# A LoRA router on one core: eight rows per load instead of four in the middle of the input stream

## The chip, the core and the metric

The kernel runs on one core of one Trainium2 chip. The metric is the device time of one execution in microseconds (us); the kernel before takes 88.85 us, the median of three runs (88.81 to 88.88). The profiled execution took 88.78 us, and its profile covers a span of 87.0 us from the first to the last instruction. All times inside the kernel below are counted from the start of that span.

## The reference

```python
def reference(x, router_weights):           # x: 16 x 512 x 1024, float32; weights: 1024 x 8
    logits = np.matmul(x, router_weights)
    exp_logits = np.exp(logits - np.max(logits, axis=-1, keepdims=True))
    return (exp_logits / np.sum(exp_logits, axis=-1, keepdims=True)).astype(np.float32)
```

There are 8192 rows of 1024 numbers. Each row is multiplied with a thin matrix of eight columns, and a softmax over the eight results is written out. The input is 33.6 MB and the output 0.26 MB.

## The kernel before

**Layout.** The 8192 rows are spread over 128 partitions, 64 consecutive rows to each (`J = 64`). "Row j" below means the 128 rows that stand at place j of their partitions, a tile of 128 x 1024. Since the 64 rows of a partition lie one after the other in memory, several rows of one partition are one contiguous piece.

**Loading.** `LOADS` (L38) says how many rows each load brings. Load 0 (rows 0 to 3) comes as float32 from the SyncE queue in two transfers of two rows (L65), and ScalarE casts it to bfloat16 row by row (L74). All other loads are issued by GpSimd (L76), and the transfer itself casts to bfloat16 on the way. Each load has a tile of its own, `x_1`, `x_2` and so on, so no load ever waits for a buffer. Row 63 comes last in two pieces, `xe_0` of six and `xe_1` of two column blocks (L86). The compiler's framework gives the GpSimd transfers eight semaphores in turn, so GpSimd's ninth transfer waits until the first has landed, the tenth for the second, and so on: eight transfers are in flight at most.

**Working on a row.** TensorE contracts over partitions, so each row tile must first be turned. `turn` (L162) transposes the eight 128x128 blocks of a row into PSUM by matmuls with the identity. `evict` (L173) copies the result back to SBUF as `xT`: on VectorE alone for rows below `NEAR` = 54, and from there on five blocks on VectorE and three on ScalarE. `project` (L114) then makes eight small matmuls with `xT` as the stationary side, which give the eight logits of each row. It runs two rows behind the transposes (one row from row 54 on).

**Order.** The loop over j is written out under a manual schedule, so each engine runs its instructions in exactly the order of the program: transposes of row j, projection of row j-2, then filler. For rows 24 to 59 `fill` (L104) adds matmuls of 128x512 on a constant tile whose result nobody reads: two per row for rows 24 to 47, one per row for rows 48 to 59. There is no filler after row 59. The softmax of a group of eight rows is cut in five steps, and one step is done after each row's eviction (L134 to L149).

**End.** After the loop come row 62, which comes in a load of its own, and row 63 from the two `xe` pieces. A transfer named `mark` waits for `xe_0`, then the first 54 rows of output are stored (L195); the last ten rows follow after the last softmax (L224).

Of the kernel before, what the change touches and what calls it, by code (L numbers as in the profile page):

```python
# [10 lines left out]
def kernel(  # L11
# [23 lines left out]
    ALU = mybir.AluOpType  # L35


    LOADS = [4] * 13 + [2, 2, 2] + [1] * 5  # L38
    LAST_LOADS = [6, 2]
    GROUPS = [8] * 6 + [6, 8, 1, 1]  # L40
    assert sum(LOADS) == J - 1 and sum(LAST_LOADS) == KO and sum(GROUPS) == J
    DONE = sum(GROUPS[:7])
# [11 lines left out]
    with tc.manual_schedule():  # L54
# [7 lines left out]

        x_f32 = const.tile([P, LOADS[0], D], fp32)
        for k in range(0, LOADS[0], 2):
            nc.sync.dma_start(out=x_f32[:, k:k + 2, :], in_=x_rows[:, k:k + 2, :])  # L65
# [3 lines left out]
        j0 = 0  # L69
        for i, r in enumerate(LOADS):  # L70
            xb = xpool.tile([P, r, D], bf16, name=f"x_{i}", tag=f"x_{i}")
# [183 lines left out]
```

## Time and profile before

| what | before |
|---|---|
| device time | 88.85 us |
| span of the profile | 87.0 us |
| TensorE matmul busy | 63.8 us (73% of the span) |
| VectorE busy | 48.1 us (55%) |
| ScalarE busy | 12.4 us (14%) |
| GpSimd busy | 12.9 us (15%) |
| queue of the GpSimd transfers | 3168 packets, 15.73 MB written, 88.3% of the 16 DMA engines' span |
| HBM read | 33.59 MB |

The megabytes of the queue are counted on the side that writes, in bfloat16; the reading side is twice as large. Busy shares are averages over the whole span. The first 40 us, in which TensorE waits for most loads, and the last 30 us, in which it has filler to do, are different stages. The granted clock of TensorE is 0.934 of full speed on average, which is also a mixture of stretches at full and at half clock.

### The profile page before, as it was taken

The page shows a single profiled execution, that of the slowest core. Times are in us where ns is not written, and L with a number is a line of the kernel's source. Part 1 is how long each engine was busy: PE and PEld are TensorE (multiplying, and loading weights), DVE is VectorE, ACT ScalarE, POOL GpSimd, SP SyncE. Part 2 cuts the span into 40 slices and gives each one's busy share as a digit, 9 for nine tenths or more (in the row PEclk, how much of TensorE's full clock was granted, in tenths as well). Part 3 has the DMA queues.
Part 4 walks back from the last instruction along what each step waited for, and adds up shares of the span by engine and source line. Part 5 has one row for each costly group of instructions (what it writes and reads, how often), then busy time and mean ns, then how long its engine had stood idle before and what let it go on. Part 6 is the DMA issues. An engine that isn't in the chain of part 4 may idle for free.

```text
span 87.0 us, 2427 instructions
## 1 busy us (share of the span) xinstructions
PE 63.8 (73%) x1092; PEld 53.6 (62%) x1092; DVE 48.1 (55%) x112; ACT 12.4 (14%) x25; POOL 12.9 (15%) x29
## 2 busy tenths in 40 slices
PE   0408004999396926949999998989898999997730
PEld 0407004999296926947777775757575888795620
DVE  0303300699576663723677677746676589563760
ACT  3235009000100010000010001000100003454540
POOL 5990002020010202020010202020010222000000
PEclk9999999999956999555999999999999999999997
DMA  3899999999999999999999999999999999999520
GB/s 60 328 358 286 260 249 222 222 211 230 196 222 211 222 215 211 226 207 215 218 215 226 200 226 215 207 226 207 226 207 198 220 213 210 202 210 211 88 102 19
DMA packets 3773, 18.26 MB, mean 210 GB/s; under 512 B 556, under 2 KB 940, under 8 KB 1972
## 3 DMA queue, kind: packets, MB, share of 16 engines
q0 software_dynamic: 3168, 15.73, 88.3%
q1 hardware_dynamic: 580, 2.36, 7.3%
q8 instruction: 8, 0.13, 0.5%
q10 hardware_dynamic: 16, 0.03, 0.2%
q14 instruction: 1, 0.01, 0.0%
HBM read 33.59 MB, written 0.26 MB: 389 GB/s over the span
## 4 chain that ended last, share of the span: by engine, by line
DMA 89%; POOL 3%; issue 2%; DVE 1%; PE 1%; ACT 0%; POOLq 0%
DMA x<-in_x_dram 75%; DMA xe<-in_x_dram 14%; POOL x L76 2%; POOL filler L81 1%; DVE xT L173 0%; PE lg L114 0%; PE pt L162 0%; POOL ident masks.py:199 0%; ACT ev_last L215 0%; POOL ident masks.py:197 0%; DVE ssum_last L219 0%; DVE low L214 0%; DVE ssum_last L220 0%; DVE outv L221 0%; POOLq L239 0%
## 5 line engine op out<-in xcount | busy, mean ns | idle before, releaser
L173 DVE COPY xT<-pt 128x1024 bf16<-128x1024 bf16 (+2 forms) x65 | 42.0, 652 | 31.8 <-PE pt L162 31.6
L162 PE MATMUL pt<-identity,x 128*128 128x128 bf16 x504 | 43.4, 236 | 16.0 <-ACT x L74 8.1
L162 PEld LDWEIGHTS <-x 128*128 128x128 bf16 x504 | 34.6, 105 | 25.8 <-DMA x<-in_x_dram 10.9
L114 PE MATMUL lg<-w_bf,xT 128*128 128x8 bf16 x512 | 22.7, 168 | 0.3 <-DVE xT L173 0.2
L114 PEld LDWEIGHTS <-xT 128*128 128x128 bf16 x512 | 20.7, 99 | 0.5 <-DVE xT L173 0.5
L104 PE MATMUL spare<-filler 128*128 128x512 bf16 x60 | 19.2, 384 | 0.0
L76 POOL DMA_DIRECT2D x<-in_x_dram x20 | 10.7, 543 | 56.2 <-DMA x<-in_x_dram 55.4
L140 ACT ACTIVATE ev<-ex 128x64 f32<-128x64 f32 (+1 forms) x8 | 2.0, 255 | 56.2 <-DVE ex L137 56.2
L173 ACT COPY xT<-pt 128x384 bf16<-128x384 bf16 (+1 forms) x10 | 4.7, 467 | 5.1 <-PE pt L162 4.9
L74 ACT CAST x<-x_f 128x1024 bf16<-128x1024 f32 x4 | 4.0, 1042 | 8.5 <-DMA x_f<-in_x_dram 8.5
L104 PEld LDWEIGHTS <-filler 128*128 128x128 bf16 x60 | 4.1, 96 | 0.0
L92 PE MATMUL lg<-ident,w 8*128 8x8 f32 x8 | 1.0, 254 | 3.1 <-POOL ident masks.py:199 3.1
L92 PEld LDWEIGHTS lg<-ident,w 8*128 8x128 f32 x8 | 1.0, 198 | 3.1 <-POOL ident masks.py:199 3.1
L89 DVE CAST identity<-ident 128x128 bf16<-128x128 f32 x1 | 0.5, 512 | 3.0 <-POOL ident masks.py:199 3.0
L134 DVE TENSOR_REDUCE mx<-lg 128x8 f32<-128x64 f32 (+1 forms) x8 | 1.7, 213 | 0.5 <-PE lg L114 0.5
L137 DVE TENSOR_TENSOR ex<-lg,mx 128x64 f32<-128x64 f32 (+1 forms) x8 | 1.7, 213 | 0.0
L149 DVE TENSOR_TENSOR outv<-ev,inv 128x64 f32<-128x64 f32 (+1 forms) x8 | 1.7, 212 | 0.0
L143 DVE TENSOR_REDUCE ssum<-ev 128x8 f32<-128x64 f32 (+1 forms) x8 | 1.7, 208 | 0.0
L86 POOL DMA_DIRECT2D xe<-in_x_dram x2 | 1.1, 527 | 3.9 <-DMA x<-in_x_dram 3.9
L146 DVE RECIPROCAL inv<-ssum 128x8 f32<-128x8 f32 (+1 forms) x8 | 1.5, 191 | 0.0
L74 ACT ACT_TABLE_LOAD x1 | 1.3, 1283 | 1.3 <-PEq L239 1.3
L162 PE MATMUL pt<-identity,xe 128*128 128x128 bf16 x8 | 0.6, 222 | 0.2 <-DMA xe<-in_x_dram 0.2
(14 smaller groups left out, 3.4 us busy)
## 6 DMA issues: line engine op xcount, KB each, us to landing
x<-in_x_dram POOLq DMA_DIRECT2D x12, 1024.0 KB, 35.4
x_f<-in_x_dram SPq DMA_DIRECT2D x2, 1024.0 KB, 8.4
x<-in_x_dram POOLq DMA_DIRECT2D x3, 512.0 KB, 33.9
x<-in_x_dram POOLq DMA_DIRECT2D x5, 256.0 KB, 20.6
out_dram<-outv SPq DMA_DIRECT2D x1, 216.0 KB, 1.9
xe<-in_x_dram POOLq DMA_DIRECT2D x1, 192.0 KB, 11.8
xe<-in_x_dram POOLq DMA_DIRECT2D x1, 64.0 KB, 9.7
out_dram<-outv SPq DMA_DIRECT2D x1, 40.0 KB, 1.5
```

Source lines behind the costliest of these rows:

```text
L74: nc.scalar.copy(xb[:, k, :], x_f32[:, k, :])
L76: nc.gpsimd.dma_start(out=xb[:], in_=x_rows[:, j0:j0 + r, :])
L92: nc.tensor.transpose(w_ps[:, n, :], w8[:, :, n], ident[0:KO, 0:KO])
L104: nc.tensor.matmul(spare[:], lhsT=filler[:, 0:P], rhs=filler[:], start=True, stop=True)
L114: nc.tensor.matmul(logits[g][:, k, :], lhsT=xT[:, i, :], rhs=w_bf[:, k0 + i, :], start=(k0 + i == 0), stop=(k0 + i == KO - 1),)
L134: nc.vector.reduce_max(mx[:, :, 0], lg, axis=X)
L137: nc.vector.tensor_tensor(out=ex[:], in0=lg, in1=mx[:].broadcast_to([P, n, N]), op=ALU.subtract)
L140: nc.scalar.activation(ev[:], ex[:], func=Exp)
L143: nc.vector.reduce_sum(ssum[:, :, 0], ev[:], axis=X)
L149: nc.vector.tensor_tensor(out=outv[:, a:a + n, :], in0=ev[:], in1=inv[:].broadcast_to([P, n, N]), op=ALU.mult)
L162: nc.tensor.transpose(pt[:, c, :], xb[:, (i + c) * P:(i + c + 1) * P], identity[:])
L173: copy(out=xT[:], in_=pt[:, 0:n, :])
```

## The change

One line is changed.

```diff
-    LOADS = [4] * 13 + [2, 2, 2] + [1] * 5
+    LOADS = [4] + [8] * 5 + [4] * 2 + [2, 2, 2] + [1] * 5
```

Rows 4 to 43 came in ten loads of four rows (16 KB contiguous per partition in memory, 8 KB after the cast). They now come in five loads of eight rows (32 KB contiguous, 16 KB after the cast). The aim is fewer and longer pieces for the DMA engines. Rows 0 to 3 and everything from row 44 on are loaded in the same pieces as before. GpSimd issues 17 transfers instead of 22; with eight in flight at most, rows 4 to 53 are now in flight at the start, where it was rows 4 to 35. The order of the instructions on TensorE, VectorE and ScalarE is the same as before; only the load that a row waits for is another one.

## The prediction

> **What bounds the kernel now.** I read the chain that ended last first. It is nearly all transfers:
>
> ```profile
> DMA 89%; POOL 3%; issue 2%; DVE 1%; PE 1%; ACT 0%; POOLq 0%
> DMA x<-in_x_dram 75%; DMA xe<-in_x_dram 14%; POOL x L76 2%; POOL filler L81 1%; DVE xT L173 0%; PE lg L114 0%; PE pt L162 0%; POOL ident masks.py:199 0%; ACT ev_last L215 0%; POOL ident masks.py:197 0%; DVE ssum_last L219 0%; DVE low L214 0%; DVE ssum_last L220 0%; DVE outv L221 0%; POOLq L239 0%
> ```
>
> So the kernel ends when the last input lands, plus a short tail. How close is TensorE behind? GpSimd's timeline is a clock of the landings: each issue after the eighth waits for a load and starts 0.28 us after it (columns: start, duration, engine, line, operation, count, idle before).
>
> ```profile
> 48.23 0.53 POOL L76 DMA_DIRECT2D x<-in_x_dram  x1 [4.34 <-DMA x<-in_x_dram]
> 53.16 0.53 POOL L76 DMA_DIRECT2D x<-in_x_dram  x1 [4.40 <-DMA x<-in_x_dram]
> 58.01 0.53 POOL L76 DMA_DIRECT2D x<-in_x_dram  x1 [4.32 <-DMA x<-in_x_dram]
> 62.90 0.53 POOL L76 DMA_DIRECT2D x<-in_x_dram  x1 [4.37 <-DMA x<-in_x_dram]
> ```
>
> Rows 32-35 have landed at 47.95, rows 40-43 at 57.73, rows 44-47 at 62.62: four rows per 4.87. TensorE's timeline over the same stretch, rows 40, 41 and 44:
>
> ```profile
> 57.77 0.62 PE L162 MATMUL pt<-identity,x 128*128 128x128 bf16 x8 [0.36 <-DMA x<-in_x_dram]
> 58.23 0.34 PE L114 MATMUL lg<-w_bf,xT 128*128 128x8 bf16 x8
> 58.43 0.59 PE L104 MATMUL spare<-filler 128*128 128x512 bf16 x2
> 58.86 0.61 PE L162 MATMUL pt<-identity,x 128*128 128x128 bf16 x8
> ...
> 62.66 0.51 PE L162 MATMUL pt<-identity,x 128*128 128x128 bf16 x6 [0.40 <-DMA x<-in_x_dram]
> ```
>
> This carries the prediction. A row costs TensorE 58.86 - 57.77 = 1.08 us, filler included; four cost 4.33 of the 4.87 us in which they arrive. It waits only 0.4 us per load, so in this stage it can make up 0.54 us per load and no more. The last stage, same view, rows 48, 61, 62 and 63:
>
> ```profile
> 67.57 0.62 PE L162 MATMUL pt<-identity,x 128*128 128x128 bf16 x8 [0.41 <-DMA x<-in_x_dram]
> ...
> 79.97 0.62 PE L162 MATMUL pt<-identity,x 128*128 128x128 bf16 x8 [0.47 <-DMA x<-in_x_dram]
> ...
> 81.31 0.61 PE L162 MATMUL pt<-identity,x 128*128 128x128 bf16 x8
> 82.16 0.64 PE L162 MATMUL pt<-identity,xe 128*128 128x128 bf16 x8 [0.24 <-DMA xe<-in_x_dram]
> ```
>
> TensorE still waits for loads at rows 61 and 63: it is caught up. Last, the clock, by stretches (length, busy time of each engine, then PEclk):
>
> ```profile
> 17.46:24.29 6.83, 5.34 (x134) 5.25 (x131) 5.44 (x11) 0.26 (x1) 0.99 (x2) 1.00 1.01 212
> 24.29:27.70 3.41, 3.30 (x53) 3.21 (x49) 2.67 (x7) 0.00 (x0) 0.07 (x1) 0.50 1.04 216
> 27.70:31.11 3.41, 2.74 (x64) 2.65 (x64) 2.55 (x6) 0.00 (x0) 0.53 (x1) 1.00 1.02 214
> 41.35:82.10 40.75, 38.26 (x662) 29.66 (x659) 27.45 (x65) 5.20 (x14) 4.22 (x8) 1.00 1.04 209
> ```
>
> **What the Trainium skill says.** "DMA: Bandwidth & Descriptors", section Anatomy of one DMA: a GpSimd transfer has about 2 us of fixed cost, mostly the receipt of its last write. Here that is hidden, as later loads stand queued behind: in the trace's packet records an undisturbed DMA engine finishes its four-row loads every 4.867 us, two-row loads every 2.457, one-row loads every 1.252. The differences, 2.410 and 1.205, are exactly proportional to rows, which leaves 0.047 us fixed per load. Same page, section Why small descriptors are slow: an overhead of some three cycles per packet. The trace agrees that it is small: the 0.047 covers eight packets and a completion. Same page, section Queues, rings and completion order: an engine alternates between queues packet by packet. The trace agrees: from 5.2 to 12 us packets of the second float32 transfer and of `x_1` alternate, one pair per 0.925 us. "TensorE: Matmul & The Clock Gate", Part 1: the clock is set by how busy TensorE was in a free-running window of about 3.4 us, else it is halved. The 3.41 us steps above agree. The window 27.70 to 31.11 with 2.74 us busy kept the clock; the one ending at 24.29, with an idle gap of 1.49, lost it.
>
> **The change, part by part.**
>
> *Removed: five loads.* 5 x 0.047 = 0.24 us off the stream, all of it gone by the time row 43 lands; later loads keep their spacing. The lower bound is 0, if the hardware cuts 32 KB pieces in two. The upper bound comes from packet durations: an 8 KB packet takes 625 ns and a 4 KB one 324, so some 23 ns are not proportional; 40 packets fewer per engine x 23 ns + 5 completions x 22 ns = 1.0 us. I take 0.24, since intervals count the overlap of packets and durations do not. GpSimd's 5 x 0.53 us of issuing saved cost nothing before: it waited 55.4 us at L76.
>
> *Start.* Packets of `x_1` become twice as long (about 1.2 us), so each pair takes about 1.5 and the second float32 transfer lands near 17.3 instead of 13.09. ScalarE's casts (1.04 each) and TensorE's rows 2 and 3 move behind it; rows 4-11 follow at about 20.7 and, at 0.65 to 1.07 each, end by 26 to 29. Rows 12-19 come at 28.2, so this is hidden.
>
> *Moved: the first row of each pair of loads waits for the second four.* Rows 4, 12, 20, 28 and 36 become available about 4.9 us later than before. For the first four blocks the slack swallows it: eight rows arrive per 9.69 us. Rows 20-27 may run partly at half clock, as rows 20-26 do now. For rows 28-35 the work is 8 x 1.08 = 8.65, so they begin at 47.95 - 0.2 and end by 56.4, before the next block.
>
> *The last block is not swallowed.* Rows 36-43 are free at 57.73 - 0.24 + 0.04 = 57.53; row 36 began at 52.92 before. From there TensorE has, by the spacing of its own rows where they did not wait:
> - rows 36-47: 12 x 1.08 = 12.97 (rows 44-47 have landed at 62.4, before their turn at 66.2)
> - rows 48-53: six in 67.57 to 72.78 = 5.21 (one filler each, 0.87 per row)
> - row 54, where one extra projection is flushed: 1.07
> - rows 55-59: five at 0.87 = 4.34
> - row 60, without filler: 0.68, from 0.45 transposes and 0.2 projection
> - row 61, whose projection waits for its own eviction: 1.34 (79.97 to 81.31)
>
> The sum is 25.61, so row 62 begins at 57.53 + 25.61 = 83.14 instead of 81.31: 1.83 later. All loads have landed by then (row 62 before 81.2, `xe` before 82.5), so TensorE never waits again after 57.5. The wait for data at the end is replaced by a queue of work: behind row 36 all later rows queue on TensorE, and VectorE, ScalarE and the last store wait for them. VectorE does not bind in the block (0.69 copy + about 0.13 softmax per row against 1.08 or 0.87). The tail after row 62 is the same chain, paced by ScalarE's copies from 82.17 on. 88.85 + 1.83 = 90.7.
>
> **Rivals.** *Half clock in the backlog, slower still.* Before row 36 TensorE idles about 0.9 us, leaving 2.5 busy in a window, between the 2.74 that kept the clock and the 1.92 (3.41 - 1.49) that lost it. If it is lost, one window of 3.41 us runs rows at 1.90 (rows 24 to 25 now) instead of 1.08: 3.41 x (1 - 1.08/1.90) = 1.5 us more, 92.2. Against it: a gap split by a window's edge counts less, and continuous work follows.
>
> *The stream alone sets the end: faster.* If TensorE caught up, only the shorter stream would show: 88.85 - 0.24 = 88.6, or 87.9 at the upper bound. For it speaks the chain, 89% transfers. Against it: this needs 1.8 us of slack after row 36, and 25.6 us of fixed work up to row 62 against the 23.4 us from row 43's landing to row 62's (57.73 to 81.17) show none; nothing in the change shortens filler.
>
> *A wash.* The saving is 1.0 us and TensorE recovers another 0.8: 88.9. The bound alone gives 57.73 - 1.0 and thus 89.9.
>
> **How the numbers follow.** Late TensorE at full clock, 90.7: 0.70. Half clock, 92.2: 0.20. Stream alone, 88.6: 0.08. Wash: 0.02. The range runs from the first case with the upper saving (89.9, less 0.2 for the landing of row 43, which hangs on the slowest DMA engine, 1.4 us behind the first) to the half-clock case with no saving at all (92.4): 89.7 to 92.4. It leaves out the last two cases.
>
> **What would show it.** Right: landings of rows 43 and 47 some 0.24 us earlier; row 36 at about 57.5; no wait of TensorE for loads after that; row 62 near 83.1; transfers no longer dominating the end of the chain. Wrong: gaps for loads at rows 56 to 63 (the stream still bounds); eight-row landings not 9.69 us apart (the saving is mis-sized); half clock after 57 us (the second case).

## The result and the profile after

The changed kernel takes 90.38 us (median of five runs, 90.14 to 90.44) against 88.84 us before (five runs, 88.81 to 88.88). The ratio is 1.0166, with a 95% interval of 1.0153 to 1.0180: 1.54 us slower, where 1.83 was forecast. The profiled execution has a span of 88.5 us. In the experiments below, two executions (91.77 us with four long loads, 93.73 us with one long load alone) fell in a slower state; the ratios leave them out.

The chain that ended last, by engine and by line:

```profile
DMA 49%; PE 39%; POOL 3%; DVE 2%; issue 2%; another core or an unknown queue 1%; ACT 0%; POOLq 0%
DMA x<-in_x_dram 49%; PE pt L162 18%; PE spare L104 12%; PE lg L114 8%; POOL x L76 2%; DVE xT L173 1%; POOL filler L81 1%; POOL ident masks.py:199 0%; ACT ev_last L215 0%; DVE mx L134 0%; DVE ex L137 0%; POOL ident masks.py:197 0%; DVE ssum_last L219 0%; DVE ssum_last L220 0%
```

Transfers had 89% of it; now they have 49%, and TensorE has 39%: transposes, filler and projections. `xe` is gone from the chain. The pieces of the chain in order of time change from the input to TensorE at 47.66 us, which is row 28. But the view does not name what ended the wait before row 36:

```profile
56.48 0.94 another core or an unknown queue
57.47 0.62 PE pt L162 x8
```

The load of rows 36 to 43 landed at 57.42 (below), so the wait was for this load, and TensorE's own work leads to the end from row 36 on. The 39% are too high by rows 28 to 35.

GpSimd's timeline again tells the landings (each issue follows one by 0.28 us; the lines tell of rows 28-35, 36-43 and 44-47):

```profile
47.90 0.53 POOL L76 DMA_DIRECT2D x<-in_x_dram  x1 [9.19 <-DMA x<-in_x_dram]
57.70 0.53 POOL L76 DMA_DIRECT2D x<-in_x_dram  x1 [9.27 <-DMA x<-in_x_dram]
63.41 0.53 POOL L76 DMA_DIRECT2D x<-in_x_dram  x1 [5.18 <-DMA x<-in_x_dram]
```

Row 43 has landed at 57.42 instead of 57.73, but row 47 at 63.12 instead of 62.62. TensorE's timeline for rows 36 and 37 and for the end, rows 61, 62 and 63. (Some matmul records are missing, so a filler pair can show as x1; the start times are whole.)

```profile
57.47 0.62 PE L162 MATMUL pt<-identity,x 128*128 128x128 bf16 x8 [0.99 <-DMA x<-in_x_dram]
57.92 0.34 PE L114 MATMUL lg<-w_bf,xT 128*128 128x8 bf16 x8
58.34 0.38 PE L104 MATMUL spare<-filler 128*128 128x512 bf16 x1
58.55 0.61 PE L162 MATMUL pt<-identity,x 128*128 128x128 bf16 x8
...
81.67 0.61 PE L162 MATMUL pt<-identity,x 128*128 128x128 bf16 x8
...
82.99 0.61 PE L162 MATMUL pt<-identity,x 128*128 128x128 bf16 x8
...
83.43 0.50 PE L162 MATMUL pt<-identity,xe 128*128 128x128 bf16 x6
```

Row 36 waits 0.99 us for its load, and it is the last that does. Rows 61 and 63 had waited in the kernel before; here `xe_0` had landed 1.5 us before its transposes began. The waits between 57 and 84 us confirm it: the only matmul that waits for a load is that one.

```profile
PE pt L162 <- DMA x<-in_x_dram: 1.0, 1, 1.0
```

The clock, by stretches (the granted clock is the third number from the end of a line). The second line is the 3.4 us window around the idle time before row 28:

```profile
42.51:82.10 39.59, 36.36 (x644) 29.57 (x654) 27.10 (x62) 4.52 (x12) 3.17 (x6) 1.00 1.01 205
45.92:49.34 3.42, 2.05 (x33) 1.44 (x33) 1.43 (x4) 0.26 (x1) 0.53 (x1) 1.00 1.09 232
```

The clock was full from 42.51 on, so the half-clock rival did not happen in this execution. The five executions lie within 0.3 us of each other, so none of them has the extra 1.5 us of that rival either.

### The profile page after: what moved, and what is told of

The parts are those of the page before. It is cut to its first block, busy times and chain, and to the rows that moved or that the text cites. A ratio compares the mean times of both kernels' runs of the same rounds, so it can differ in the third digit from the quotient of the medians.

```text
span 88.5 us, 2410 instructions
## 1 busy us (share of the span) xinstructions
PE 61.0 (69%) x1080; PEld 53.1 (60%) x1092; DVE 48.0 (54%) x112; ACT 12.3 (14%) x25; POOL 10.3 (12%) x24
## 4 chain that ended last, share of the span: by engine, by line
DMA 49%; PE 39%; POOL 3%; DVE 2%; issue 2%; another core or an unknown queue 1%; ACT 0%; POOLq 0%
DMA x<-in_x_dram 49%; PE pt L162 18%; PE spare L104 12%; PE lg L114 8%; POOL x L76 2%; DVE xT L173 1%; POOL filler L81 1%; POOL ident masks.py:199 0%; ACT ev_last L215 0%; DVE mx L134 0%; DVE ex L137 0%; POOL ident masks.py:197 0%; DVE ssum_last L219 0%; DVE ssum_last L220 0%
## 5 line engine op out<-in xcount | busy, mean ns | idle before, releaser
L162 PE MATMUL pt<-identity,x 128*128 128x128 bf16 x504 | 42.9, 235 | 19.8 <-ACT x L74 12.7
L104 PE MATMUL spare<-filler 128*128 128x512 bf16 x48 | 15.5, 377 | 0.6
L76 POOL DMA_DIRECT2D x<-in_x_dram x15 | 8.1, 549 | 58.6 <-DMA x<-in_x_dram 57.9
```

The lines of the kernel that those rows point to most:

```text
L76: nc.gpsimd.dma_start(out=xb[:], in_=x_rows[:, j0:j0 + r, :])
L104: nc.tensor.matmul(spare[:], lhsT=filler[:, 0:P], rhs=filler[:], start=True, stop=True)
L162: nc.tensor.transpose(pt[:, c, :], xb[:, (i + c) * P:(i + c + 1) * P], identity[:])
```

## The experiments

All times are medians. Ratios, with 95% intervals, are against the kernel before, which was run beside each group on the same chip and took 88.94 us (beside four long loads, one long load alone, one filler from row 36, and loads of two), 88.89 (beside three long loads, no filler, and six more fillers in either kernel) and 88.91 (beside the filled gap). "Late" means later than in the profile of the kernel before.

**Which of the long loads matters.** First only the last pair of short loads is put back:

```diff
-    LOADS = [4] + [8] * 5 + [4] * 2 + [2, 2, 2] + [1] * 5
+    LOADS = [4] + [8] * 4 + [4] * 4 + [2, 2, 2] + [1] * 5
```

> Rows 4 to 35 in four loads of eight, rows 36 to 43 again in two loads of four; nothing else differs from the changed kernel. Theory (TensorE is late because rows 36 to 39 wait for rows 40 to 43, and it can then make up only 0.54 us per four rows): row 36 starts near 52.7 again, TensorE is caught up at the end and waits for rows 60 to 63, and only the shorter stream shows: 88.84 - 4 x 0.047 = 88.65 us. Rival (longer pieces as such make the late stage slower, in proportion to their number): four fifths of the 1.54 us remain, 90.1 us.

It took 89.32 us, ratio 1.0041 (1.0019 to 1.0064): the miss is mine. TensorE's timeline, rows 28, 48 and 62:

```profile
48.11 0.62 PE L162 MATMUL pt<-identity,x 128*128 128x128 bf16 x8 [1.04 <-DMA x<-in_x_dram]
...
69.72 0.61 PE L162 MATMUL pt<-identity,x 128*128 128x128 bf16 x8
...
82.28 0.61 PE L162 MATMUL pt<-identity,x 128*128 128x128 bf16 x8
```

Row 36 did not start at 52.7 but at 56.76, since rows 28-35 were themselves a late block: their load landed at 48.07 (0.3 later than by the interval count; this execution took 89.58 us), and eight rows of 1.08 us end after the next four rows have landed at 52.93. TensorE never waited again from row 28 on: 20 rows x 1.08 = 21.6 us to row 48, which is 2.15 late, and row 62 is 0.97 late (1.68 in the changed kernel). So a long load makes TensorE late as soon as shorter ones follow, whichever load it is: row 36 began 3.84 us later than before, which is the 4.9 us less the 1.04 us idle before row 28. What counts is how many rows are left to make it up. The proportional rival (90.1) is outside the interval too.

So the revised rule was tried with the last long load one place earlier:

```diff
-    LOADS = [4] + [8] * 5 + [4] * 2 + [2, 2, 2] + [1] * 5
+    LOADS = [4] + [8] * 3 + [4] * 6 + [2, 2, 2] + [1] * 5
```

> Rows 4 to 27 in three loads of eight, rows 28 to 51 in six loads of four. Revised theory (the last load of eight leaves TensorE late by about 4.9 us less its idle time, and each later load of four takes back 0.54 us): row 20 starts near 38.1, row 28 near 46.9, row 48 near 68.5 where it could start at 67.5, and TensorE is caught up at row 61, just in time; the stream saves 3 x 0.047: 88.7 us, up to 88.9 with the scatter of the slowest DMA engine. Rival (the 0.38 us that remained with four loads of eight shrinks in proportion to their number): 89.2 us.

It took 88.89 us, ratio 0.9990 (0.9973 to 1.0006). Row 20 started at 38.10, row 28 at 47.12, row 48 at 68.72 and row 61 at 79.92, where its load had landed at 79.80: caught up just in time, as the rule says. The line of row 61 shows no wait any more:

```profile
79.92 0.61 PE L162 MATMUL pt<-identity,x 128*128 128x128 bf16 x8
```

Row 28 was 3.22 us late and row 48 still 1.15: five loads of four took back about 2.1 us, and rows 54 to 60 the rest. The interval leaves out 89.2.

**One long load alone, and a filled gap.** Now the reverse: rows 4 to 35 as before, one load of eight for rows 36 to 43.

```diff
-    LOADS = [4] * 13 + [2, 2, 2] + [1] * 5
+    LOADS = [4] * 9 + [8] + [4] * 2 + [2, 2, 2] + [1] * 5
```

> Only rows 36 to 43 come in one load of eight; rows 4 to 35 stay in loads of four. Theory: nearly the whole loss comes with this one load, and the stream saves 0.047 instead of 0.24 us: row 36 starts near 57.7, row 62 near 83.2, 90.38 + 0.19 = 90.6 us. Rival (in proportion to the number of long loads): one fifth of the loss, 89.15 us.

It took 92.83 us, ratio 1.0392 (1.0346 to 1.0439): more than the whole loss. The median is 2.2 us beyond the theory, the interval of the ratio 1.4 to 2.2 us. TensorE's timeline, rows 36 to 39, and the clock by stretches (third number from the end):

```profile
57.73 1.03 PE L162 MATMUL pt<-identity,x 128*128 128x128 bf16 x8 [4.74 <-DMA x<-in_x_dram]
...
59.62 1.06 PE L162 MATMUL pt<-identity,x 128*128 128x128 bf16 x8
...
61.54 1.06 PE L162 MATMUL pt<-identity,x 128*128 128x128 bf16 x8
...
63.17 0.61 PE L162 MATMUL pt<-identity,x 128*128 128x128 bf16 x8
```

```profile
42.40:56.05 13.65, 10.36 (x173) 7.94 (x173) 7.81 (x17) 0.51 (x2) 1.05 (x2) 1.00 1.02 215
56.05:62.88 6.83, 4.92 (x52) 3.93 (x54) 1.86 (x5) 0.00 (x0) 0.53 (x1) 0.50 1.04 217
```

This is the half-clock rival of the prediction. Here TensorE was caught up, so it stood idle for 4.74 us before row 36, the clock was halved at 56.05, and rows 36 to 38 took 1.89, 1.92 and 1.64 us: 2.2 more than 3 x 1.08. In the changed kernel the long load before it had kept TensorE busy until shortly before row 36.

If that is so, useless work in the gap must make this kernel with one long load faster:

```diff
-                fill(2 if j < 48 else 1)
+                fill(22 if j == 35 else 2 if j < 48 else 1)
```

> The kernel in which only rows 36 to 43 come in one load of eight, with 20 more fillers after row 35: 20 x 0.216 = 4.3 us of work that nobody needs, put into the 4.9 us in which TensorE waited for that load. Theory (the extra 2.2 us of that kernel over the forecast of 90.6 are rows at half clock after the idle gap): the clock stays full, rows 36 to 38 take 1.08 us each, and the time falls to 90.6 us. Rival (the extra time is something else about that load): it stays at 92.8 us.

It took 90.99 us, ratio 1.0229 (1.0203 to 1.0256). TensorE's timeline, the filler after row 35, then rows 36 and 37:

```profile
52.12 4.91 PE L104 MATMUL spare<-filler 128*128 128x512 bf16 x21
58.58 0.62 PE L162 MATMUL pt<-identity,x 128*128 128x128 bf16 x8 [1.56 <-DMA x<-in_x_dram]
59.04 0.34 PE L114 MATMUL lg<-w_bf,xT 128*128 128x8 bf16 x8
...
59.67 0.61 PE L162 MATMUL pt<-identity,x 128*128 128x128 bf16 x8
```

The clock stayed full across the gap:

```profile
42.40:57.50 15.10, 14.35 (x186) 9.60 (x186) 7.80 (x17) 0.51 (x2) 1.06 (x2) 1.00 1.02 217
```

From row 36 to row 62 it took 25.50 us instead of 27.72. Added work of 4.3 us took 1.8 us off the median. The profiled execution (91.38 us) is the slowest of the four; its load of row 36 landed at 58.54, not 57.68, and that much later TensorE began. Whether late landings also explain the 0.4 us by which the median lies over the forecast was not seen in the unprofiled runs.

**Is the backlog made of filler?** One filler instead of two after rows 36 to 47 of the changed kernel; the filler's result is not read by anything.

```diff
-                fill(2 if j < 48 else 1)
+                fill(2 if j < 36 else 1)
```

> The changed kernel's loads, with one filler instead of two after each of rows 36 to 47; the filler's result is not used, so the output is the same. Theory (a backlog of fixed TensorE work): the 12 rows take 0.87 instead of 1.08 us each, 2.6 us less than the 1.83 us by which row 62 was late, so TensorE catches up before row 62 and the stream sets the end: 88.84 - 0.24 = 88.6 us. Rival (the transfers, not TensorE's work, set the end): no change from 90.4 us.

(Row 62 was late by 1.68 us in the profile; 1.83 was the forecast. Either is less than the 2.6 us taken out.) It took 88.83 us, ratio 0.9992 (0.9980 to 1.0004). The loss is gone: TensorE is caught up and waits for rows 61 and 63 again.

```profile
79.77 0.62 PE L162 MATMUL pt<-identity,x 128*128 128x128 bf16 x8 [0.34 <-DMA x<-in_x_dram]
...
81.10 0.61 PE L162 MATMUL pt<-identity,x 128*128 128x128 bf16 x8
81.98 0.94 PE L162 MATMUL pt<-identity,xe 128*128 128x128 bf16 x8 [0.27 <-DMA xe<-in_x_dram]
```

The stream's 0.24 us did not come with it; the interval allows at most 0.18. Rows 61 and 62 were 0.20 earlier than before, but the second piece of row 63 landed at 82.59 instead of 82.47, and the transposes of row 63 stretch to 0.94 us for it.

Then all filler was removed from the changed kernel (`fill(0)` in that line).

> The changed kernel's loads with no filler at all; the filler's result is not used, so the output is the same. Theory (the backlog is made of filler): a row costs 0.65 us at full clock and 1.07 at half clock, so eight rows fit into the 9.69 us of a load either way and TensorE is caught up; 88.7 us if the clock is full in the tail, 89.6 if it is half there, since the last transposes and projections then take twice as long. Rival (the landings set the end of the changed kernel): 90.4 us or more.

It took 88.86 us, ratio 0.9990 (0.9969 to 1.0011). The clock fell to half in four stretches, the last one 75.14 to 78.55, and was full again in the tail; rows cost 0.65 or 1.07 us, and row 61 waited for its load. Again the transfers set the end.

**Slack before, none after.** The same six fillers are added to both kernels.

```diff
-                fill(2 if j < 48 else 1)
+                fill(3 if 36 <= j < 42 else 2 if j < 48 else 1)
```

> The changed kernel with one more filler after each of rows 36 to 41 (three instead of two). Theory (no slack is left after row 36): all six count, 6 x 0.216 = 1.3 us, 91.7 us. Rival (TensorE still waits for something after row 36): less than that, down to 90.4 us.

> The kernel before with the same six fillers added after rows 36 to 41. Theory (slack of 0.54 us per load of four): row 42 starts 0.8 us late, row 44 0.2 us late, row 48 on time; no change, 88.85 us. Rival (TensorE's work counts in the kernel before too): 1.3 us more, 90.1 us.

The changed kernel took 91.71 us, ratio 1.0311 (1.0279 to 1.0344): 1.33 more than 90.38, where 1.30 was added. The kernel before took 88.85, ratio 0.9993 (0.9983 to 1.0003). In the first, rows 36 and 37 are 1.31 apart, and row 62 starts 1.24 later than in the changed kernel:

```profile
57.43 0.62 PE L162 MATMUL pt<-identity,x 128*128 128x128 bf16 x8 [0.95 <-DMA x<-in_x_dram]
...
58.74 0.61 PE L162 MATMUL pt<-identity,x 128*128 128x128 bf16 x8
...
84.23 0.61 PE L162 MATMUL pt<-identity,x 128*128 128x128 bf16 x8
```

In the second, rows 42, 44 and 48 began 1.02, 0.46 and 0.14 us later than before, of which row 36 already had 0.27: the lateness shrinks from load to load, as expected. Row 61 waits for its load as ever:

```profile
80.09 0.62 PE L162 MATMUL pt<-identity,x 128*128 128x128 bf16 x8 [0.41 <-DMA x<-in_x_dram]
```

This pair is the plainest test of where the bound is.

**The price of a load.** In the other direction, rows 4 to 43 of the kernel before in twenty loads of two:

```diff
-    LOADS = [4] * 13 + [2, 2, 2] + [1] * 5
+    LOADS = [4] + [2] * 20 + [4] * 2 + [2, 2, 2] + [1] * 5
```

> The other way: rows 4 to 43 in twenty loads of two rows instead of ten of four; filler as before. TensorE gets rows earlier, not later, so only the stream shows. Theory (0.047 us fixed per load on each DMA engine): 10 x 0.047 = 0.47 more, 89.3 us. Rival (packet durations count in full: 80 more packets per engine at 23 ns and 10 completions at 22 ns): 2.1 us more, 90.9 us.

It took 89.60 us, ratio 1.0060 (1.0041 to 1.0079), which is 0.36 to 0.70 us more: the 0.47 of the interval count lies inside, the 2.1 of the duration count far outside. In the packet records the first engine finishes one of these loads every 2.46 us.

## Why the prediction was right

**The stream.** Eight-row loads came 9.69 us apart on an undisturbed DMA engine (completion packets of the first engine: 26.58, 36.27, 45.96, 55.64), as worked out from 0.047 us per load. Packets of 16 KB took 1227 ns, against 2 x 625, so their durations shrank as the upper bound assumed. But eight of them sum to 9.82 us, more than the interval: the durations overlap, and taking the intervals was the right choice. One sign failed: row 47 landed 0.50 us later instead of 0.24 earlier. Fifteen of the sixteen completions of its load were in by 62.28, the last came at 63.12. It cost nothing, since row 44 had its turn only at 66.11.

**The start.** The second float32 transfer landed at 17.79 (forecast 17.3) and row 2 began at 18.92. Rows 4-11 began from 21.07 on and ended at 26.6, before the next load at 28.77. Hidden, as said. One reading of the kernel before was inexact: the half clock from 34.53 to 41.35 covers mainly rows 22 to 25, not 20 to 26; nothing in the forecast rests on it.

**The late block.** Row 36 began at 57.47 (forecast 57.53). That this fits to 0.06 us is in part luck: with the same loads, row 43 landed at 57.39, 57.42, 57.60 and 57.73 in four profiles (six more fillers, the changed kernel, one filler from row 36, no filler). Row 62 came 25.52 us after it (forecast 25.61), at 82.99. Without a wait in between, the sum was fixed work, and the filler experiments show that this work was the loss: 12 fillers fewer remove it, six more add their own 1.3 us.

**What was mis-sized.** The step "the tail after row 62 is the same chain, paced by ScalarE's copies" was 0.17 us off. In the kernel before, row 63's transposes began 0.85 us after row 62's, since `xe_0` had only just landed; here they followed after 0.44. The final store was issued 3.14 us after row 62's start instead of 3.31. With the 0.06 of row 36 and the 0.09 of the sum, this makes the forecast 1.83 into the 1.51 us between the final stores in the two profiles (84.62 and 86.13).

**The rivals.** The half-clock rival was a real mechanism, as one long load alone shows. In the profiled execution of the changed kernel the clock was kept, even in its emptiest window since 42.51 (before row 28, 2.05 us of work in 3.42). "The stream alone" fell with the pair of six fillers, and so did "A wash": row 43 came 0.31 us earlier and not 1.0, and TensorE made up nothing after it. The weak place of my reasoning was not in the prediction but in the first experiment: I took the fourth long load as harmless since the changed kernel showed a wait behind it. That wait was there only because the next load was long as well.

## What to carry to other kernels

In these kernels work on a row waits until the whole of its load has landed, so joining two loads delays the first half by the time of the second. Before making loads longer, take that delay less the time the consumer stood idle, divide it by what the consumer can make up per load (here 4.9 us, less the idle time, by 0.54) and count the loads that are left; put the long ones early, where enough loads are left to make it up. Deliberate filler eats exactly the slack that would absorb such a delay, and whether an engine has slack is quickly tested by adding a known amount of work to it.

## What I had not expected

The saving of the stream did not show in the time. Three variants in which TensorE was caught up, with 0.14 to 0.24 us less stream by the interval count, took 88.83, 88.89 and 88.86 us, none apart from the kernel before by its interval; no version beat it. Only the first interval (one filler from row 36) leaves out the forecast saving; the other two are too wide to tell. The landing of a load is that of its slowest DMA engine, which before and after the change passes row 43 some 1.4 us after the first one. In two kernels with the same loads (one long load alone, without and with the filled gap) row 43 landed at 57.68 and 58.54. The packet records show eight packets of 16 KB on the instruction queue, 0.89 to 0.98 us each, and in the kernel before a packet of input took some 0.2 us longer than its like soon after nearly each of them; and with nearly each fetch one more of the sixteen completions of a load came 0.6 us or more later than the others. That these fetches, and the DMA engine that each falls on, decide the last landing is argued from the records, not tested.

The busy time in one window does not settle whether the clock is kept. In the changed kernel a window with 2.05 us of work in 3.42 kept it, and in the kernel before one with 1.92 lost it, but other runs cross these figures: with loads of two the window 61.44 to 64.85 kept the clock with 1.66 us of work, and without filler the one from 71.73 to 75.14 lost it with 1.96. The forecast of the half-clock case, which placed 2.5 us between 2.74 and 1.92, thus had a weak base; what decides stays open.

"TensorE: Matmul & The Clock Gate", Part 4 of the Trainium skill, says that transposes in TensorE's transpose mode do not engage the full clock, since they do not count as busy in the same way. The kernel without filler does not bear that out for its transposes, which are matmuls with the identity: with them and eight-column projections alone the clock was full from 61.49 to 75.14, and the projections are only about 0.2 of the 0.65 us of a row. Whether these transposes run in the mode that the page means, the traces do not show.
